# State-space blocks with rows ordered (channel, token) instead of (token, channel), in an encoder trunk on one core

## The chip, the core and the metric

The kernel runs on one core of a Trainium2 chip. The core has a matrix engine (PE), a vector engine (DVE), a scalar engine (ACT), a general engine (POOL) and a sync engine (SP) that issues nearly all DMAs here. The metric is the time of one execution on the device in microseconds (us); lower is better. Every time below is from executions of the kernel before.

## What is computed

Two layers over 512 tokens of width 1024, in float32. Layer 0 is dilated-window attention, layer 1 a bidirectional S5 state-space layer; each is followed by a SwiGLU feed-forward block, and a last norm ends it. The change lies in the state-space layer (64 groups of 16 channels, 64 complex states in each direction):

```python
u = (hn @ w_in).astype(jnp.float32).reshape(b, s, SSM_GROUPS, SSM_GROUP_CH)
y = d_skip.astype(jnp.float32).reshape(SSM_GROUPS, SSM_GROUP_CH) * u
for direction in range(SSM_DIRS):
    y = y + s5_direction(u, a_re[direction], a_im[direction], log_dt[direction], ...,
                         reverse=(direction == 1))
y = jax.nn.gelu(y.reshape(b, s, SSM_WIDTH)).astype(hn.dtype)
ag = y @ w_glu
return ag[..., :D_MODEL] * jax.nn.sigmoid(ag[..., D_MODEL:])
```

`s5_direction` computes `bur, bui = einsum(u, B-bar)`, runs the recurrence `x[t] = lambda x[t-1] + bu[t]` over the tokens and returns `Re(C x)`.

## The kernel before

**Large products.** Every weight matrix is cut into units of 128 output columns. A unit is loaded into `wraw` (SP, L88, L93 or L96) and split into a rounded high part `whi` (ACT, L116) and a remainder `wlo` (L117, on DVE, or on POOL in the state-space stage). A product is then three matmuls per block of 128 x 128 weights: xhi with whi, xlo with whi, xhi with wlo, 24 for a unit of eight blocks. `wraw`, `whi` and `wlo` have three buffers each; loads run three units ahead and splits two. Eight units, those of `w_ssm_in`, are listed in `swap`: they are split with their 128 columns exchanged from (group, channel) to (channel, group), so both instructions (L113, L114) read `wraw` with a step of 16 elements, 64 bytes.

**Tables of the state-space layer.** While PE multiplies the first feed-forward block (FFN0: gps and ups are its gate and up products, fps its output), the class `Tables` builds, for each of the eight tiles T of 128 channels (8 groups), what the state-space stage needs: Ti (input table), ph (phases), Bt (output table) and Mt (the part within a block of 8 tokens). They are cut into pieces; a planner (`Bg`) hands pieces out between the FFN0 matmuls by due time, and all of an engine's work stays in the order in which it was written. `elem_in` (L440 to L442, on DVE) makes `Tn`, the product of powers `pin` (in SBUF, laid out as 8 steps l by 2 by 64 groups) and `bbP` (in PSUM), three instructions of 512 elements for each part: 2 for the halves s of a tile, 2 for real and imaginary part, 8 tiles, 32 sets. Line L440 puts its result in SBUF, L441 in PSUM. `tr_in` (L470) transposes Tn on PE, and the result goes to DRAM (`TinD`, L489). `elem_out` and `elem_ph` run on POOL, `elem_z` on ACT, and `band` (L479 to L484) makes the block for Mt, stored by four DMAs into `MD` (L501). In FFN0, DVE also works for the products themselves: g and u (L1198, L1200, L1202), hl (L1206), wlo; ACT makes g's activation (L1199) and hh (L1205).

**The state-space stage** (about 1030 to 1180 us). A product sps per tile T (24 matmuls), then: `s_u` multiplies sps by the norm factors into `u` (DVE, L1415); `s_move` moves u into the buffer `U` (SP, L1419), which holds 128 rows, one for each token l of a block of 8 and each of 16 channels, by 8 groups by 64 blocks j; `s_v` is 32 small matmuls V, four for each group (L1308); `s_scan` multiplies by ph, scans and multiplies again (DVE L1326 to L1339, POOL L1328 and L1340); ACT copies the state x (L1350, L1352); `s_out` is yps, with Mt on U (L1373) and Bt on x (L1375); then gelu, transposes and the products with w_glu. U has three buffers, u two. SP's queue holds, in one written order, the U transfers, the tables of the coming tiles (`load_tab`, L1251) and the weights. Each DMA of SP takes the next of eight lanes and waits for the one eight before it.

The rows of U are ordered (l, c) with l falling: `s_move` makes one DMA for each l, from all 128 partitions of u (64 elements each) to 16 partitions of U, all groups. With the columns of w_ssm_in exchanged, u's partitions are (c, g).

Of the kernel before, what the change touches and what calls it, by code (L numbers as in the profile page):

```python
# [7 lines left out]
F32 = mybir.dt.float32  # L8
# [62 lines left out]
class WStream:  # L71


    def __init__(self, k, units, swap, pool, la, sa):
        self.k, self.units, self.swap, self.pool, self.la, self.sa = k, units, swap, pool, la, sa
        self.nl = self.ns = self.n = 0
        self.raw, self.hl = {}, {}
        self.lo_engine = k.nc.vector
# [21 lines left out]
    def split_to(self, n):  # L100
        nc = self.k.nc
        while self.ns <= min(n, len(self.units) - 1):
# [6 lines left out]
            if self.ns in self.swap:  # L109

                src = w.rearrange("p a (g c) -> p a c g", c=16)
                h4, l4 = (t.rearrange("p (a c g) -> p a c g", a=a, c=16) for t in (hv, lv))
                nc.scalar.activation(out=h4, in_=src, func=ACTF.Copy)  # L113
                self.lo_engine.tensor_tensor(out=l4, in0=src, in1=fv(h4), op=ALU.subtract)  # L114
            else:
                nc.scalar.activation(out=hv, in_=wv, func=ACTF.Copy)  # L116
                self.lo_engine.tensor_tensor(out=lv, in0=wv, in1=fv(hv), op=ALU.subtract)  # L117
# [63 lines left out]
class Tables:  # L181
# [5 lines left out]
    def __init__(self, k, a, cst, ident, pool, dram, rho):  # L187
# [8 lines left out]
        self.MD = [dram.tile([8, 16, 8, 128], F32, name=f"MD{t}") for t in range(KT)]  # L196
# [236 lines left out]
    def elem_in(self, T, s, i):  # L433
# [3 lines left out]
        if i == 0:  # L437
            self.Tn[T, s] = self.t("Tn", [2, 4, 8, 16], 2)
        t, o = self.ptm.tile([P, 4, 8, 16], F32, tag="tm", name="tm"), self.Tn[T, s][:, i]
        tt(out=o, in0=self.bc(self.pin, 0, g0), in1=self.ch(bb[:, i]), op=ALU.mult)  # L440
        tt(out=t, in0=self.bc(self.pin, 1, g0), in1=self.ch(bb[:, 1 - i]), op=ALU.mult)  # L441
# [21 lines left out]
    def tr_in(self, T, s, q):  # L463
# [4 lines left out]
        for g in range(2):  # L468
            for i in range(2):
                nc.tensor.transpose(ps[:, g, i, :], self.Tn[T, s][:, i, 2 * q + g].rearrange("p l c -> p (l c)"), self.ident)  # L470
# [26 lines left out]
    def store_e(self, T, s):  # L497

        for k_ in range(4):
            e = self.E[32 * k_:32 * k_ + 16, :]  # L500
            self.nc.sync.dma_start(out=self.MD[T][:, :, 4 * s + k_, :].rearrange("l c x -> c l x"),  # L501
# [40 lines left out]
def build(tc, a, out):  # L542
# [45 lines left out]
    swap = range(len(units), len(units) + KT)  # L588
# [31 lines left out]
    with ExitStack() as ctx:  # L620
# [4 lines left out]
        ws = WStream(k, units, swap, wpool, 3, 2)  # L625
# [620 lines left out]
        def load_tab(T, *names):  # L1246
            for n in names:
                shape, src = {"Ti": ([8, 2, 128], tabs.TinD[T]), "ph": ([2, S], tabs.PhD[T]), "Bt": ([2, 8, 128], tabs.BD[T]),
                              "Mt": ([8, 128], tabs.MD[T].rearrange("l c g x -> (l c) g x"))}[n]
# [163 lines left out]
        def s_u(T, ps, rB):  # L1413
            us[T] = sp.tile([P, S], F32, tag="u", name="u", bufs=2)
            nc.vector.tensor_tensor(out=us[T], in0=ps, in1=rB, op=ALU.mult)  # L1415
# [224 lines left out]
```

## Time and profile of the kernel before

| what | us |
|---|---|
| median of 3 runs | 1630.33 |
| range of the runs | 1623.66 to 1632.44 |
| the profiled execution | 1624.28 |
| its span in the trace | 1622.4 |
| PE busy in it | 1527.7 |
| DVE, ACT, POOL busy | 976.6, 660.6, 452.5 |

The profile is of one execution; 1.9 us of its time lie outside the span. The mean granted clock of PE is 0.979 of full speed. Busy time is an average over very different stages, so a change is read from the stretch that it touches: the idle time of PE there, the instruction that ended it, and the instructions that this one waited for in turn. Names such as `wlo<-wraw,whi` give output and inputs; L117 is a line of the kernel before.

### The profile page before, as it was taken

What the parts mean: (1) busy time and instruction counts of PE and PEld (TensorE: products, weight loads), DVE (VectorE), ACT (ScalarE), POOL (GpSimd) and SP (SyncE); (2) the same over time, 40 slices, a digit from 0 to 9 for tenths busy, and PEclk for the clock granted to TensorE, in tenths of its full rate; (3) what the DMA queues carried; (4) which work ended last, traced back from release to release, by engine and by line L of the source; (5) the groups of instructions that cost most, each with busy time, mean ns of one, the idle gap of its engine ahead of it and who ended that gap; (6) DMA issues with size and microseconds to landing.
All of it is one profiled execution on the core that took longest, in us unless ns stands there. A gap on an engine that the chain in (4) does not pass through costs nothing. (4 is left out here: it accounts for less than half of the span.)

```text
span 1622.4 us, 22425 instructions
## 1 busy us (share of the span) xinstructions
PE 1527.7 (94%) x8428; PEld 1261.1 (78%) x8428; DVE 976.6 (60%) x1721; ACT 660.6 (41%) x1172; POOL 452.5 (28%) x535
## 2 busy tenths in 40 slices
PE   8999999999998889799999999887799999999997
PEld 6887888898897668677777777776587888888886
DVE  6366665665666478888578875486547443344234
ACT  5265454454564323244344444442433333233122
POOL 1022001010110250387666754464413101101010
PEclk9999999999999899999999999998999999999999
DMA  6322232231222033355566547467623332333332
GB/s 185 91 78 58 62 92 64 78 87 58 90 68 66 29 86 91 84 143 146 166 194 175 163 145 253 146 223 218 210 70 88 104 103 80 104 98 98 105 102 65
DMA packets 279180, 185.16 MB, mean 114 GB/s; under 512 B 39936, under 2 KB 261280, under 8 KB 277024
## 3 DMA queue, kind: packets, MB, share of 16 engines
q1 hardware_dynamic: 278640, 183.13, 38.3%
q8 instruction: 66, 1.08, 0.3%
q10 hardware_dynamic: 432, 0.60, 0.1%
q14 instruction: 42, 0.34, 0.1%
HBM read 154.34 MB, written 27.26 MB: 112 GB/s over the span
## 5 line engine op out<-in xcount | busy, mean ns | idle before, releaser
L117 DVE TENSOR_TENSOR wlo<-wraw,whi 128x1024 fp32r<-128x1024 f32 (+1 forms) x232 | 312.1, 1349 | 192.7 <-ACT whi L116 191.0
L116 ACT ACTIVATE whi<-wraw 128x1024 fp32r<-128x1024 f32 x238 | 241.1, 1018 | 236.1 <-PE ops L1599 74.3
L789 PE MATMUL gps<-xhi,whi 128*128 128x512 f32 x792 | 320.2, 404 | 9.5 <-DVE hl L1206 6.5
L789 PE MATMUL gps<-xhi,wlo 128*128 128x512 f32 x792 | 311.9, 394 | 7.0 <-DVE wlo L117 7.0
L789 PE MATMUL gps<-xlo,whi 128*128 128x512 f32 x792 | 310.6, 392 | 0.5 <-DVE xlo L649 0.5
L983 POOL COPY st<-st 32x4 f32<-32x4 f32 x256 | 59.7, 233 | 453.9 <-ACT P L971 337.9
L789 PEld LDWEIGHTS gps<-xhi,wlo 128*128 128x128 f32 x792 | 149.3, 189 | 43.7 <-DVE wlo L117 11.2
L789 PEld LDWEIGHTS gps<-xhi,whi 128*128 128x128 f32 x792 | 149.6, 189 | 39.7 <-ACT whi L116 10.0
L789 PEld LDWEIGHTS gps<-xlo,whi 128*128 128x128 f32 x792 | 149.9, 189 | 26.0 <-DVE xlo L649 0.8
L789 PE MATMUL ups<-xhi,wlo 128*128 128x512 f32 x352 | 138.1, 392 | 2.0 <-DVE wlo L117 2.0
L789 PE MATMUL ups<-xhi,whi 128*128 128x512 f32 x352 | 139.6, 397 | 0.0
L789 PE MATMUL ups<-xlo,whi 128*128 128x512 f32 x352 | 137.7, 391 | 0.0
L971 ACT ACTIVATE P<-P,st 128x256 f32<-128x256 f32 x128 | 63.8, 499 | 68.7 <-DVE st L968 68.6
L1202 POOL TENSOR_TENSOR u<-u,g 128x512 f32<-128x512 f32 x22 | 28.4, 1291 | 209.7 <-DVE u L1200 202.2
L789 PEld LDWEIGHTS ups<-xhi,wlo 128*128 128x128 f32 x352 | 66.4, 189 | 17.0 <-DVE wlo L117 2.8
L452 POOL TENSOR_TENSOR B<-pout,C 128x512 f32<-128x512 f32 x32 | 45.3, 1415 | 122.4 <-DVE pout L178 64.3
L789 PEld LDWEIGHTS ups<-xhi,whi 128*128 128x128 f32 x352 | 66.5, 189 | 14.5 <-issue 1.2
L789 PEld LDWEIGHTS ups<-xlo,whi 128*128 128x128 f32 x352 | 66.6, 189 | 13.4
L1199 ACT ACTIVATE g<-g 128x512 f32<-128x512 f32 x44 | 27.7, 630 | 115.2 <-DVE g L1198 115.2
L789 PE MATMUL fps<-hh,whi 128*128 128x512 f32 x176 | 71.4, 406 | 3.4 <-ACT hh L1205 2.7
L891 PE MATMUL vps<-whi,xhi 128*128 128x256 f32 x256 | 73.3, 286 | 0.0
L1205 ACT ACTIVATE hh<-u 128x512 fp32r<-128x512 f32 x44 | 27.8, 633 | 109.9 <-POOL u L1202 87.7
(303 smaller groups left out, 3163.1 us busy)
## 6 DMA issues: line engine op xcount, KB each, us to landing
wraw<-in_w_ffn_in SPq DMA_DIRECT2D x88, 512.0 KB, 3.8
wraw<-in_w_qkv SPq DMA_DIRECT2D x72, 512.0 KB, 3.6
wraw<-in_w_ffn_out SPq DMA_DIRECT2D x38, 512.0 KB, 4.0
BD<-B SPq DMA_DIRECT2D x16, 512.0 KB, 5.3
TinD<-Tt SPq DMA_DIRECT2D x16, 512.0 KB, 3.5
Ti<-TinD SPq DMA_DIRECT2D x8, 1024.0 KB, 6.0
Bt<-BD SPq DMA_DIRECT2D x8, 1024.0 KB, 7.3
wraw<-in_w_attn_out SPq DMA_DIRECT2D x8, 512.0 KB, 3.8
```

Source lines behind the costliest of these rows:

```text
L116: nc.scalar.activation(out=hv, in_=wv, func=ACTF.Copy)
L117: self.lo_engine.tensor_tensor(out=lv, in0=wv, in1=fv(hv), op=ALU.subtract)
L452: tt(out=B[:, i], in0=self.bc(self.pout, i, g0), in1=self.ch(C[:, 0]), op=ALU.mult)
L789: nc.tensor.matmul(dst, w[:, kt, :], x, start=(start and kt == ks[0] and j == 0), stop=(stop and kt == ks[-1] and j == 2))
L891: nc.tensor.matmul(ps[rp][:, r % 2, :], x, w[:, kk, :], start=(kt == 0 and j == 0 and r % 2 == 0), stop=(kt == 7 and j == 2 and r % 2 == 1))
L971: nc.scalar.activation(out=Pt[:, j, :], in_=Pt[:, j, :], func=ACTF.Exp, bias=st[:, 32 + off + j:33 + off + j], accum_out=st[:, 8 + off + j ...
L983: nc.gpsimd.tensor_copy(par[32 * z:32 * z + 32, y, :, :], own[32 * y:32 * y + 32, z, :, :])
L1199: nc.scalar.activation(out=g, in_=g, func=ACTF.Silu)
L1202: eng.tensor_tensor(out=u, in0=u, in1=g, op=ALU.mult)
L1205: nc.scalar.activation(out=hi, in_=u, func=ACTF.Copy)
```

## The change

The rows of U, of Ti and of Mt go from (l, c) to (c, l).

- The columns of w_ssm_in keep their order: `swap` is gone, and all units are split by the contiguous instructions. The partitions of u are then (g, c).
- `s_u` writes u with the eight blocks of 64 tokens in reverse, by a negative step between blocks; still one instruction.
- `s_move` makes one DMA for each group g: from 16 partitions of u (8 blocks of 64 elements each) to all 128 partitions of U at that group. Again eight DMAs of 32 KB in pieces of 256 bytes for a tile.
- `elem_in` makes Tn as (group, c, l). pin is read with l as the inner index, 128 elements (512 bytes) apart, and each set is repeated for the 16 c; bbP is repeated for the 8 l. Before, pin was repeated for c (inner) and bbP read along c.
- `MD` is laid out (c, l), so `store_e` writes 128 rows of 512 bytes in order; `load_tab` reads Mt accordingly.

The diff, without the places where the parameter `swap` is passed on:

```diff
@@ -106,15 +106,8 @@
             lo = self.pool.tile([P, 1024], F32R, tag="wlo", name="wlo")
             hv, lv = (t[:, 0:a * b] for t in (hi, lo))
             wv = w.rearrange("p a b -> p (a b)")
-            if self.ns in self.swap:
-
-                src = w.rearrange("p a (g c) -> p a c g", c=16)
-                h4, l4 = (t.rearrange("p (a c g) -> p a c g", a=a, c=16) for t in (hv, lv))
-                nc.scalar.activation(out=h4, in_=src, func=ACTF.Copy)
-                self.lo_engine.tensor_tensor(out=l4, in0=src, in1=fv(h4), op=ALU.subtract)
-            else:
-                nc.scalar.activation(out=hv, in_=wv, func=ACTF.Copy)
-                self.lo_engine.tensor_tensor(out=lv, in0=wv, in1=fv(hv), op=ALU.subtract)
+            nc.scalar.activation(out=hv, in_=wv, func=ACTF.Copy)
+            self.lo_engine.tensor_tensor(out=lv, in0=wv, in1=fv(hv), op=ALU.subtract)
             self.hl[self.ns] = tuple(t.rearrange("p (a b) -> p a b", a=a) for t in (hv, lv))
             self.ns += 1
 
@@ -193,7 +186,7 @@
         self.TinD = [dram.tile([P, 8, 2, 128], F32, name=f"TinD{t}") for t in range(KT)]
         self.BD = [dram.tile([P, 2, 8, 128], F32, name=f"BD{t}") for t in range(KT)]
         self.PhD = [dram.tile([P, 2, S], F32, name=f"PhD{t}") for t in range(KT)]
-        self.MD = [dram.tile([8, 16, 8, 128], F32, name=f"MD{t}") for t in range(KT)]
+        self.MD = [dram.tile([16, 8, 8, 128], F32, name=f"MD{t}") for t in range(KT)]
         self.z, self.C = {}, {}
 
     def scratch(self, n, cols):
@@ -435,10 +428,13 @@
         g0 = 8 * T + 4 * s
         bb = self.bbP[:, :, 4 * s:4 * s + 4]
         if i == 0:
-            self.Tn[T, s] = self.t("Tn", [2, 4, 8, 16], 2)
-        t, o = self.ptm.tile([P, 4, 8, 16], F32, tag="tm", name="tm"), self.Tn[T, s][:, i]
-        tt(out=o, in0=self.bc(self.pin, 0, g0), in1=self.ch(bb[:, i]), op=ALU.mult)
-        tt(out=t, in0=self.bc(self.pin, 1, g0), in1=self.ch(bb[:, 1 - i]), op=ALU.mult)
+            self.Tn[T, s] = self.t("Tn", [2, 4, 16, 8], 2)
+        t, o = self.ptm.tile([P, 4, 16, 8], F32, tag="tm", name="tm"), self.Tn[T, s][:, i]
+
+        pw = [self.pin[:, :, j, g0:g0 + 4].rearrange("p l (g o) -> p g o l", o=1).to_broadcast([P, 4, 16, 8]) for j in range(2)]
+        b = [bb[:, j].rearrange("p g (c o) -> p g c o", o=1).to_broadcast([P, 4, 16, 8]) for j in range(2)]
+        tt(out=o, in0=pw[0], in1=b[i], op=ALU.mult)
+        tt(out=t, in0=pw[1], in1=b[1 - i], op=ALU.mult)
         tt(out=o, in0=o, in1=t, op=(ALU.subtract, ALU.add)[i])
 
     def elem_out(self, T, s):
@@ -467,7 +463,7 @@
         ps = self.psb.tile([P, 2, 2, 128], F32, tag="b", name="tps")
         for g in range(2):
             for i in range(2):
-                nc.tensor.transpose(ps[:, g, i, :], self.Tn[T, s][:, i, 2 * q + g].rearrange("p l c -> p (l c)"), self.ident)
+                nc.tensor.transpose(ps[:, g, i, :], self.Tn[T, s][:, i, 2 * q + g].rearrange("p c l -> p (c l)"), self.ident)
         nc.scalar.activation(out=self.Tt[:, 2 * q:2 * q + 2], in_=ps, func=ACTF.Copy)
 
     def band(self, T, s):
@@ -498,7 +494,7 @@
 
         for k_ in range(4):
             e = self.E[32 * k_:32 * k_ + 16, :]
-            self.nc.sync.dma_start(out=self.MD[T][:, :, 4 * s + k_, :].rearrange("l c x -> c l x"),
+            self.nc.sync.dma_start(out=self.MD[T][:, :, 4 * s + k_, :],
                                    in_=bass.AP(tensor=e.tensor, offset=e.offset, ap=[list(e.ap[0]), [16, 8], [1, 128]]))
 
     def pieces(self):
@@ -1246,7 +1241,7 @@
         def load_tab(T, *names):
             for n in names:
                 shape, src = {"Ti": ([8, 2, 128], tabs.TinD[T]), "ph": ([2, S], tabs.PhD[T]), "Bt": ([2, 8, 128], tabs.BD[T]),
-                              "Mt": ([8, 128], tabs.MD[T].rearrange("l c g x -> (l c) g x"))}[n]
+                              "Mt": ([8, 128], tabs.MD[T].rearrange("c l g x -> (c l) g x"))}[n]
                 t = tbx2[0].tile([P] + shape, F32, tag=n, name=n, bufs=2)
                 nc.sync.dma_start(out=t, in_=src)
                 ld.setdefault(T, {})[n] = t
@@ -1412,11 +1407,16 @@
 
         def s_u(T, ps, rB):
             us[T] = sp.tile([P, S], F32, tag="u", name="u", bufs=2)
-            nc.vector.tensor_tensor(out=us[T], in0=ps, in1=rB, op=ALU.mult)
-
-        def s_move(T, lo_=0, hi_=8):
-            for l in range(lo_, hi_):
-                nc.sync.dma_start(out=Us[T % 3][112 - 16 * l:128 - 16 * l, :, 1:65], in_=us[T][:, 64 * l:64 * l + 64])
+            u = us[T]
+            v = lambda x: x.rearrange("p (l j) -> p l j", l=8)
+
+            nc.vector.tensor_tensor(out=bass.AP(tensor=u.tensor, offset=u.offset + 448, ap=[list(u.ap[0]), [-64, 8], [1, 64]]),
+                                    in0=v(ps), in1=v(rB), op=ALU.mult)
+
+        def s_move(T):
+
+            for g in range(8):
+                nc.sync.dma_start(out=Us[T % 3][:, g, 1:65], in_=us[T][16 * g:16 * g + 16].rearrange("c (l j) -> c l j", l=8))
 
         ws.lo_engine = nc.gpsimd
         late = []
```

What this does to the order of work. On PE, at the V matmuls of tile T = 1 (they read U and Ti), the kernel before has this; DMAHW0 to 7 are SP's eight lanes:

```order
L789 MATMUL sps_9704<-xlo_9456,whi 128x512
L789 MATMUL sps_9704<-xhi_9455,wlo 128x512
L1308 MATMUL V<-U_9485,Ti 64x64 [waits DMAHW3_49,DMAHW4_49,DMAHW2_49,DMAHW5_49,DMAHW1_49,DMAHW6_49,DMAHW0_49,DMAHW7_49,DVE_49,PE_49]
L1308 MATMUL V<-U_9485,Ti 64x64 x31
L1373 MATMUL yps<-Mt,U_9484 64x128 x2
```

and the changed kernel this:

```order
L784 MATMUL sps_9704<-xlo_9456,whi 128x512
L784 MATMUL sps_9704<-xhi_9455,wlo 128x512
L1303 MATMUL V<-U_9485,Ti 64x64 [waits DMAHW3_49,DVE_49,PE_49]
L1303 MATMUL V<-U_9485,Ti 64x64 x3
L1303 MATMUL V<-U_9485,Ti 64x64 [waits DMAHW4_49]
L1303 MATMUL V<-U_9485,Ti 64x64 x3
```

One wait for eight transfers at the first matmul has become a wait for one transfer ahead of each group's four matmuls; 28 of the tile's 32 matmuls can run before its last transfer has landed.

On SP, at the transfers of u into U for tile T = 3, the first that use a U buffer again (yps of T = 0, on PE, has to have read it), the kernel before has:

```order
L1251 DMA ph<-PhD_5475 128x1024 [waits DMAHW6_49,DVE_49]
L1419 DMA U_9484<-u 16x8x64 [waits DMAHW7_49,DVE_49,PE_49]
L1419 DMA U_9484<-u 16x8x64 [waits DMAHW0_49]
L1419 DMA U_9484<-u 16x8x64 [waits DMAHW1_49]
L1419 DMA U_9484<-u 16x8x64 [waits DMAHW2_49]
```

and the changed kernel:

```order
L1246 DMA ph<-PhD_5475 128x1024 [waits DMAHW6_49,DVE_49]
L1419 DMA U_9484<-u 128x1x64 [waits DMAHW7_49,DVE_49,PE_49]
L1419 DMA U_9484<-u 128x1x64 [waits DMAHW0_49,PE_49]
L1419 DMA U_9484<-u 128x1x64 [waits DMAHW1_49,PE_49]
L1419 DMA U_9484<-u 128x1x64 [waits DMAHW2_49,PE_49]
L1419 DMA U_9484<-u 128x1x64 [waits DMAHW3_49]
L1419 DMA U_9484<-u 128x1x64 [waits DMAHW4_49]
L1419 DMA U_9484<-u 128x1x64 [waits DMAHW5_49]
L1419 DMA U_9484<-u 128x1x64 [waits DMAHW6_49,PE_49]
L1246 DMA Mt<-MD_5483 128x1024 [waits DMAHW7_49]
```

Before, the first transfer waits for PE and the others for their lanes alone; after, transfers 0 to 3 and 7 each wait for PE's reads of their own group. The loads of Mt and of what follows stand in the same place behind them.

## Rows read from the trace of the kernel before

**Rows 1.** The page, part 1: busy us (share of the span) and instructions, by engine.

```profile
PE 1527.7 (94%) x8428; PEld 1261.1 (78%) x8428; DVE 976.6 (60%) x1721; ACT 660.6 (41%) x1172; POOL 452.5 (28%) x535
```

**Rows 2.** Table by stretches: start:end, length, busy us by engine, clock, DMA share, GB/s.

```profile
690.00:1000.00 310.00, 299.69 (x1529) 233.13 (x1529) 237.26 (x284) 136.28 (x248) 207.67 (x140) 0.99 0.58 164
853.00:966.00 113.00, 107.26 (x554) 83.44 (x554) 93.39 (x113) 49.75 (x92) 77.98 (x52) 1.00 0.57 159
1150.00:1180.00 30.00, 22.45 (x156) 18.43 (x157) 12.53 (x14) 14.06 (x22) 13.61 (x8) 0.83 0.53 144
```

**Rows 3.** Waits of PE, 680 to 1000 us: total us, times, longest us.

```profile
PE gps L789 <- DVE hl L1206: 6.5, 1, 6.5
PE gps L789 <- DVE wlo L117: 4.6, 5, 1.7
```

**Rows 4.** Timeline of PE: start, length, instruction, idle time before it and its releaser.

```profile
853.34 0.50 PE L789 MATMUL gps<-xhi,wlo 128*128 128x512 f32 x1 [0.40 <-DVE wlo L117]
...
966.12 0.50 PE L789 MATMUL fps<-hh,whi 128*128 128x512 f32 x1 [2.75 <-ACT hh L1205]
```

**Rows 5.** Waits of DVE, 819 to 967 us, and below from 689 to 819 us.

```profile
DVE u L1202 <- ACT g L1199: 9.9, 4, 2.5
DVE hl L1206 <- ACT hh L1205: 7.7, 11, 0.7
DVE wlo L117 <- ACT whi L116: 5.2, 9, 1.2
...
DVE wlo L117 <- ACT whi L116: 29.8, 12, 6.4
```

**Rows 6.** Groups of DVE by line, 819 to 966.1 us: busy us, mean ns, idle before.

```profile
L440 DVE TENSOR_TENSOR Tn<-pin,bbP 128x512 f32<-128x512 f32 x16 | 10.8, 678 | 0.0
L441 DVE TENSOR_TENSOR tm<-pin,bbP 128x512 f32<-128x512 f32 x16 | 11.0, 687 | 0.0
```

**Rows 7.** Single lines: count, then nanoseconds min/median/max, first and last start, forms.

```profile
L113 ACT ACTIVATE whi<-wraw x8: 1916/2008/2032, 1021.9 to 1083.3; 128x1024 fp32r<-128x1024 f32 x8
...
L114 POOL TENSOR_TENSOR wlo<-wraw,whi x6: 2860/2900/2921, 1033.2 to 1089.3; 128x1024 fp32r<-128x1024 f32 x6
L114 DVE TENSOR_TENSOR wlo<-wraw,whi x2: 1960/1968/1977, 1023.9 to 1027.1; 128x1024 fp32r<-128x1024 f32 x2
...
L117 DVE TENSOR_TENSOR wlo<-wraw,whi x232: 548/1225/2486, 16.9 to 1598.2; 128x1024 fp32r<-128x1024 f32 x100, 128x384 fp32r<-128x384 f32 x16
...
L412 POOL TENSOR_TENSOR ph<-AB x16: 1459/1582/2452, 681.5 to 983.5; 128x512 f32<-128x512 f32 x16
...
L452 POOL TENSOR_TENSOR B<-pout,C x32: 1102/1159/2176, 672.0 to 961.3; 128x512 f32<-128x512 f32 x32
```

**Rows 8.** Waits of PE from 1000 to 1180 us.

```profile
PE yps L1375 <- ACT x L1352: 17.8, 12, 5.3
PE pe L789 <- ACT gpart L1479: 7.6, 1, 7.6
PE rsps L672 <- DVE rcol L667: 0.7, 1, 0.7
```

**Rows 9.** Timelines of PE and DVE around the first V.

```profile
1050.08 3.49 PE L1308 MATMUL V<-U,Ti 128*64 128x64 f32 x64 [3.46 <-DMA U<-u]
...
1050.25 0.69 DVE L1415 TENSOR_TENSOR u<-sps,rsB 128x512 f32<-128x512 f32 x1 [6.49 <-DMA U<-u]
1053.60 0.69 DVE L1326 TENSOR_TENSOR t<-V,ph 128x512 f32<-128x512 f32 x1 [2.66 <-PE V L1308]
```

**Rows 10.** Waits of SP, DVE and ACT, 1000 to 1180 us, and the U transfers' line.

```profile
SPq L1419 <- PE yps L1373: 4.9, 1, 4.9
...
DVE t L1326 <- DMA ph<-PhD: 16.6, 4, 7.5
...
ACT whi L116 <- DMA wraw<-in_w_glu: 31.1, 4, 13.1
...
L1419 SPq DMA_DIRECT2D U<-u x64: 547/597/1647, 1043.2 to 1140.5; - x64
```

More of the change, by code (lines that the diff above doesn't have):

```diff
@@ L71, with __init__ @@
 class WStream:
-    def __init__(self, k, units, swap, pool, la, sa):
-        self.k, self.units, self.swap, self.pool, self.la, self.sa = k, units, swap, pool, la, sa
+    def __init__(self, k, units, pool, la, sa):
+        self.k, self.units, self.pool, self.la, self.sa = k, units, pool, la, sa
         self.nl = self.ns = self.n = 0
@@ L587, in build @@
             units.append(col(a["w_ffn_out"][0], m * 128, 128, half * HALF + 8, HALF - 8))
-    swap = range(len(units), len(units) + KT)
     for m in range(KT):
@@ L624, in build @@
         ctx.enter_context(tc.manual_schedule())
-        ws = WStream(k, units, swap, wpool, 3, 2)
+        ws = WStream(k, units, wpool, 3, 2)
         cst = left.tile([P, NCONST], F32, name="cst")
```

## Prediction

> **What bounds the kernel now.** The page comes first: TensorE (PE) is busy 94% of the span and DVE, the next, 60% [rows 1]. So a change gains where PE stands idle and loses where it makes PE idle. The table by stretches says where that is [rows 2]. The change touches two places: FFN0 up to 1000 us, beside which the state-space tables are built, and the state-space stage, about 1030 to 1180 us. From 690 to 1000 us PE is busy 299.69 of 310 us. In the second stage it is busy 22.45 of the 30 us from 1150 on, at a granted clock of 0.83.
>
> The sums of waits then name what PE lacks. Around FFN0 it is one wait of 6.5 us for DVE's hl and five for DVE's wlo, 4.6 us [rows 3], and smaller ones; two of the stalls are shown where they stand [rows 4]. In the state-space stage PE waits 17.8 us for the state x from ACT, 7.6 us for gpart, 0.7 us before rsps [rows 8], and 3.46 us before the first V for U's transfers [rows 9]: 29.6 us in all. Behind x and gpart stands a chain over other engines: DVE waits 16.6 us for the table ph and ACT 31.1 us for w_glu, whose loads both stand in SP's queue, and SP itself waits 4.9 us for yps to release a U buffer [rows 10]. So that stage is paced by SP's queue about as much as by DVE.
>
> **Part 1, the exchange of columns goes.** The eight units of w_ssm_in are split by contiguous instructions. A swapped unit took 1.968 us on DVE against 1.225 for a plain one, 0.74 us less for each of two units; POOL's six took 2.900 and ACT's eight 2.008 us [rows 7], and I take about the same saving for these. No unit of them is waited for by PE from 1000 us on [rows 8], so nearly all of it lies beside PE's work. What it can give directly is the 0.7 us before rsps, since DVE's rcol chain stands behind two of these subtractions. I count 0.7 us, and ends of 0 and 0.7.
>
> **Part 2, U by groups.** Before, the first V matmul of each T waits for all eight U transfers; after, the four matmuls of each group wait for that group's transfer. A batch is eight transfers of 32 KB in 256-byte pieces either way, and one issue takes 0.6 us on SP [rows 10]. At T = 0 the V matmuls start at 1050.08 and run 3.49 us [rows 9]. After, seven eighths of them, 3.49 x 7/8 = 3.05 us, run while later transfers land. DVE's t follows V [rows 9], but u(2) of 0.69 us now meets it and takes 0.4 us back. With the 0.7 of part 1 that is 3.05 + 0.7 - 0.4 = **3.4 us**, the lower end of what this stage gains if the transfers cost the same.
>
> The upper end is SP's. Before, the first transfer of U(3) waits until yps(0) has read the whole buffer (4.9 us [rows 10]); after, transfers 0 to 3 and 7 wait for their own group, as the order shows. U(3) then goes out while yps(0) runs, and the loads of Mt, Bt, w_ssm_in, Ti, ph and w_glu queued behind it go out up to 4.9 + 3.4 = 8.3 us earlier. Who waits for these is DVE (ph, 16.6 us) and ACT (w_glu, 31.1 us). What is late next: DVE's own work, and the load lanes, in which each transfer waits for the one eight before it. I put the upper end at 10 us, a third of PE's 29.6 us of waiting, and take **6.5 us**, about the middle, since two of the four waits (V and x) are moved directly. No row of before shows a transfer from 16 partitions to 128; the nearest, the present one, issues in 0.547 to 1.647 us, median 0.597 [rows 10]. I take no extra cost because count and size of the pieces stay; at +0.2 us an issue, SP would carry 64 x 0.2 = 12.8 us more in this stage, at -0.2 as much less.
>
> **Part 3, Tin's rows in the order (c, l).** The first two instructions of every set in elem_in, L440 and L441, now read pin with an inner step of 128 elements (512 bytes), where the same element was repeated over c. There are 64 of them (8 T, 2 halves, 2 parts, 2 each), at 0.678 and 0.687 us [rows 6]. No row shows this read on DVE. The nearest is DVE's subtraction with an input at a 64-byte step: 1.968 against 1.225 us for 1024 elements [rows 7], 0.726 ns per element, 0.37 us for 512. On POOL, elem_ph has the same 512-byte inner step and a median of 1.582 us against 1.159 for elem_out with the repeated element [rows 7], both beside DVE's traffic: a factor 1.36, or 0.25 us on 0.68. Bounds: 0 (the operand in PSUM may set the pace already) and 0.6 us (the step is eight times that of the DVE row). I take 0.37 us, the same engine and the nearest kind of read, so 64 x 0.37 = 24 us of DVE work.
>
> A rule speaks against this edit. The Trainium skill, page "SBUF — State Buffer", section "Door 1: The DMA port swizzle (why `[64,N]` ≈ `[32,N]`)", says that SBUF has lines of 16 bytes and that an access which moves on to a new line pays a penalty; it gives no size. By it the new read of pin pays on each element, and the DVE pair above (1.968 against 1.225 us) agrees; if it held for no operand beside PSUM, the sum would be that of rival (a).
>
> How much of the 24 us reaches PE? From 819 to 967 us DVE never waits for PE or a transfer: all its idle time is behind ACT's g, hh and whi [rows 5], and g and hh in turn follow DVE's own results. PE is stalled by DVE's wlo at 853.34 and, through hh, at 966.12 [rows 4], so lateness of DVE is handed to PE one to one. In that stretch there are 16 + 16 such instructions [rows 6]: 32 x 0.37 = 11.8 us. DVE's 5.2 us behind whi [rows 5] could absorb a little, where whi's own cause is a load; I take off a tenth, 0.5 us. Two more instructions stand ahead of the hl for which PE waits 6.5 us [rows 3]: 0.7 us. Sum 11.8 - 0.5 + 0.7 = **+12.0 us**. The other 30 instructions (from 688 to 812 us and behind 974) lie where DVE stands idle anyway (29.8 us behind whi from 689 to 819 us [rows 5], some 1.1 us for each of the 26 instructions there, since ACT's split waits for buffers that PE frees), and cost nothing; without that cover they are 30 x 0.37 = 11 us more. The ends for 0 and 0.6 us an instruction are 0 and 32 x 0.6 - 0.5 + 1.2 = 19.9 us. The clock there reads 1.00 with PE idle 5.7 of 113 us [rows 2], so I add nothing for it.
>
> **Part 4, at nothing.** Tn's transposes stay contiguous; the 64 stores of MD still move 128 pieces of 512 bytes each and stand in SP's queue behind a wait for DVE; u is still one instruction of 512 elements in runs of 64. No engine's order changes. If the reversed blocks of u cost 0.37 us like a strided read, eight of them are 3 us of DVE beside V.
>
> **Sum.** +12.0 - 6.5 = +5.5 us on the profiled execution of 1624.28 us. That one lies 6 us below the median of 1630.33 (runs from 1623.66 to 1632.44), so the difference is put on the median: **1635.8 us**.
>
> **Rivals.**
> (a) The new read is free beside an operand in PSUM. For: L440, with one operand in PSUM, and L441, with two, take nearly the same time [rows 6], so something else than the operands' layout may set it. Against: DVE's and POOL's pairs [rows 7]. Then only the gain counts, -3.4 to -10: 1620.3 to 1626.9 us, and with the 6.5 taken above **1623.8 us**.
> (b) Slower, by DVE's pace from 819 to 966 us: 0.6 us an instruction and only 3.4 us of gain, 19.9 - 3.4 = +16.5, **1646.8 us**. It decides from 0.45 us on: 32 x 0.45 - 0.5 + 0.9 - 6.5 = +8.3. For: DVE is busy 93.39 of 113 us there and the rest is spent behind ACT [rows 2, 5]. Against: POOL's pair gives less.
> (c) The order of U by groups does not do what it says beyond T = 0, because DVE or the lanes hold the rest: 12.0 - 3.4 = +8.6, **1638.9 us**. For: DVE waits for ph four times only [rows 10].
> (d) The U transfers issue 0.2 us slower and half of the 12.8 us reaches PE: +5.5 + 6.4 = +11.9, **1642.2 us**.
>
> **Chances.** A measurement of this kernel can tell about 0.5%, 8.1 us, from no change. The forecast has 0.37: 0.29 of it within that bound, 0.04 faster (the full gain of 10 and lateness that other idle time takes up) and 0.04 slower. (a) has 0.36, since no row shows the new read itself; half of that is beyond -8.1. (b) has 0.11, all slower; (c) 0.11, of which 0.06 slower; (d) 0.05, slower. Faster by over 0.5%: 0.04 + 0.18 = 0.22; slower: 0.04 + 0.11 + 0.06 + 0.05 = 0.26; within: the other 0.52. For eight in ten the range reaches from the better end of (a) to nearly the price of (b): 1619 to 1646 us; the forecast's own runs from 1629 to 1639.
>
> **What would show it.** L440 and L441 at about 1.05 us: at 0.68 it is (a), above 1.13 (b). PE's waits for wlo and hh between 819 and 966 us about 11 us longer, and the stall of 966.12 near 978. In the state-space stage the matmuls of V(0) spread over the landings with no single wait of 3.5 us; SP's wait for yps before U(3) gone or split; DVE's wait for ph below 16.6 and ACT's for w_glu below 31.1 us; the stretch from the first sps to the last x shorter by 3.4 to 10 us. I am wrong if FFN0's end does not move, if the U transfers issue or land slower, or if PE's waits for x do not shrink.

## The result: slower by 0.85%, with nearly twice the forecast loss and a gain about as forecast

| kernel | median us | lowest to highest | n |
|---|---|---|---|
| before | 1629.44 | 1623.66 to 1632.44 | 5 |
| changed | 1640.86 | 1637.46 to 1645.82 | 5 |

The ratio is 1.0085 with an interval of 1.0064 to 1.0107: 11.4 us slower, where 5.5 were forecast. The profiled execution of the changed kernel has a span of 1635.6 us, 13.2 more than that of before. In later sets before had medians of 1623.97 to 1627.32 and the changed kernel, measured again, 1643.02 (ratio 1.0122, 1.0105 to 1.0139), so its loss is 11 to 19 us.

To compare executions, each trace is cut at three instructions that every kernel has: the stall of PE for wlo near 688 to 694 us (A), its first sps matmul (S), and the start of the last group of eight yps matmuls of the state-space stage (G). A to S is called FFN0, S to G the stage.

| execution | A | S | G | FFN0 | stage | S to the end of the first V | G to the end |
|---|---|---|---|---|---|---|---|
| before | 688.68 | 1027.15 | 1177.75 | 338.5 | 150.6 | 26.4 | 444.7 |
| changed | 688.50 | 1048.59 | 1190.09 | 360.1 | 141.5 | 22.0 | 445.5 |

So FFN0 lost 21.6 us, the stage gained 9.1, and 0.8 were lost behind it.

**The rows of FFN0.** The table by stretches, A to S, before and then after (columns as in [rows 2]):

```profile
688.68:1027.15 338.47, 327.01 (x1645) 255.41 (x1646) 252.52 (x300) 149.51 (x264) 217.10 (x147) 0.99 0.61 178
```

```profile
688.50:1048.59 360.09, 337.43 (x1644) 260.63 (x1645) 273.80 (x300) 147.89 (x264) 215.91 (x147) 0.96 0.58 167
```

DVE has the same 300 instructions and is busy 273.80 instead of 252.52 us: 21.3 us more, and the stretch is 21.6 us longer. The added time is in the two edited lines, now L436 and L437 (count, then nanoseconds min/median/max):

```profile
L436 DVE TENSOR_TENSOR Tn<-pin,bbP x32: 1017/1072/1237, 679.8 to 997.6; 128x512 f32<-128x512 f32 x32
...
L437 DVE TENSOR_TENSOR tm<-pin,bbP x32: 1014/1073/1117, 680.7 to 998.6; 128x512 f32<-128x512 f32 x32
```

They answer to [rows 6]: 1.072 and 1.073 us against 0.678 and 0.687. What PE waits for, summed from A to S of the changed kernel (total us, times, longest), answers to [rows 3, 4]:

```profile
PE fps L784 <- ACT hh L1200: 4.5, 1, 4.5
PE gps L784 <- DVE wlo L110: 4.2, 4, 1.8
PE fps L784 <- DVE wlo L110: 4.1, 5, 1.5
PE gps L784 <- ACT whi L109: 4.0, 2, 3.3
PE fps L784 <- ACT whi L109: 3.0, 5, 1.4
PE tps L466 <- DVE Tn L438: 2.4, 2, 2.2
```

New among them is the wait for Tn. The others stood there before, 4.6 us for wlo at gps and the rest shorter:

```profile
PE fps L789 <- DVE wlo L117: 2.9, 3, 1.1
PE fps L789 <- ACT hh L1205: 2.7, 1, 2.7
PE gps L789 <- ACT whi L116: 1.2, 1, 1.2
```

Of the 21.6 us, 11.2 are more idle time of PE (338.47 - 327.01 = 11.46 before, 360.09 - 337.43 = 22.66 after) and 10.4 are longer busy time, at a lower clock; more on the clock below. The stall for hh, at 966.12 us before [rows 4], is here:

```profile
985.65 0.79 PE L784 MATMUL fps<-hh,whi 128*128 128x512 f32 x1 [4.46 <-ACT hh L1200]
```

**The rows of the stage.** The first V no longer waits 3.46 us in one piece [rows 9]. It waits four times for single transfers, the first of them being

```profile
1068.20 0.45 PE L1303 MATMUL V<-U,Ti 128*64 128x64 f32 x8 [0.17 <-DMA U<-u]
```

and the sums that answer to [rows 8, 10] are, of PE, DVE, ACT and SP from 1030 us on:

```profile
PE yps L1370 <- ACT x L1347: 14.0, 10, 3.8
PE pe L784 <- ACT gpart L1479: 8.1, 1, 8.1
...
DVE t L1321 <- DMA ph<-PhD: 9.4, 3, 5.9
...
ACT whi L109 <- DMA wraw<-in_w_glu: 28.5, 4, 13.5
...
SPq L1419 <- PE yps L1368: 3.9, 6, 0.9
```

PE's waits for x fell from 17.8 to 14.0 us and DVE's for ph from 16.6 to 9.4; those for w_glu (31.1 to 28.5) and gpart (7.6 to 8.1) hardly moved.

### The profile page after: what moved, and what is told of

It reads as the page before. It is cut to its first block, busy times and chain, and to the rows that moved or that the text cites. A ratio compares the mean times of both kernels' runs of the same rounds, so it can differ in the third digit from the quotient of the medians.

```text
span 1635.6 us, 22423 instructions
## 1 busy us (share of the span) xinstructions
PE 1536.5 (94%) x8428; PEld 1264.8 (77%) x8428; DVE 993.7 (61%) x1721; ACT 653.6 (40%) x1172; POOL 448.3 (27%) x535
## 5 line engine op out<-in xcount | busy, mean ns | idle before, releaser
L109 ACT ACTIVATE whi<-wraw 128x1024 fp32r<-128x1024 f32 x246 | 249.6, 1019 | 254.4 <-PE ops L1599 74.3
L784 PE MATMUL gps<-xhi,whi 128*128 128x512 f32 x792 | 323.4, 408 | 12.3 <-ACT whi L109 11.3
L784 PE MATMUL gps<-xhi,wlo 128*128 128x512 f32 x792 | 315.2, 398 | 6.7 <-DVE wlo L110 6.6
L784 PEld LDWEIGHTS gps<-xhi,whi 128*128 128x128 f32 x792 | 151.6, 191 | 43.4 <-ACT whi L109 13.3
L448 POOL TENSOR_TENSOR B<-pout,C 128x512 f32<-128x512 f32 x32 | 42.0, 1311 | 135.7 <-ACT C L394 71.4
L784 PE MATMUL fps<-hh,wlo 128*128 128x512 f32 x176 | 70.2, 399 | 4.1 <-DVE wlo L110 4.1
```

Source lines behind the costliest of these rows:

```text
L448: tt(out=B[:, i], in0=self.bc(self.pout, i, g0), in1=self.ch(C[:, 0]), op=ALU.mult)
L784: nc.tensor.matmul(dst, w[:, kt, :], x, start=(start and kt == ks[0] and j == 0), stop=(stop and kt == ks[-1] and j == 2))
```

## The experiments

### Is it the strided read alone, or the store of MD?

SP's issues of the MD store became dearer, which had been costed at nothing: 0.592 instead of 0.424 us. They stand ahead of the loads of w_ffn_out, and ACT's whi waits longer for these (below). So there were two suspects for FFN0.

```profile
L501 SPq DMA_DIRECT2D MD<-E x64: 313/424/439, 705.2 to 994.1; - x64
```

```profile
L497 SPq DMA_DIRECT2D MD<-E x64: 565/592/1417, 707.9 to 1016.6; - x64
```

**pin with l inner** (`e1_pin_l_inner`): the read is contiguous again, the order of Tn's rows stays changed.

```diff
-        self.pin, self.pout = self.t("pin", [8, 2, 64]), self.t("pout", [8, 2, 64])
+        self.pin, self.pout = self.t("pin", [2, 64, 8]), self.t("pout", [8, 2, 64])
+        pv = self.pin.rearrange("p j g l -> p l j g")
...
-        pw = [self.pin[:, :, j, g0:g0 + 4].rearrange("p l (g o) -> p g o l", o=1)...
+        pw = [self.pin[:, j, g0:g0 + 4].rearrange("p (g o) l -> p g o l", o=1)...
```

> The changed kernel with the powers pin stored with l as the inner index (written with a step of 8 elements by eight short instructions of the parameters), so that elem_in reads them in a row; all else as in the changed kernel. Theory 1, the strided read alone makes FFN0 late (64 x 0.39 = 25 us of DVE, handed to PE in part directly, in part through SP's queue): the two instructions fall from 1.07 to about 0.68 us, the stall of PE that is at 966 us before and at 985.7 after is back within 2 us of 966, and the time is the one of before less the gain of the state-space stage, about 1629.4 - 8 = 1621 us. Rival 2, the stores of MD in their new form (0.592 against 0.424 us an issue, 64 x 0.168 = 10.8 us of SP) make the loads of w_ffn_out late: that stall stays at about 976 and the time is about 1631 us.

Measured: 1624.43 us, ratio to before 0.9987 (0.9972 to 1.0002). The two lines are back at 0.680 and 0.689 us, and FFN0 is 344.8 us: 15.3 of the 21.6 us are gone. The single line, the stretch, and the stall for hh:

```profile
L437 DVE TENSOR_TENSOR Tn<-pin,bbP x32: 674/680/687, 684.2 to 987.4; 128x512 f32<-128x512 f32 x32
...
692.92:1037.67 344.75, 329.55 (x1644) 257.08 (x1645) 254.23 (x300) 147.72 (x264) 217.03 (x147) 0.98 0.60 175
...
976.24 0.50 PE L785 MATMUL fps<-hh,whi 128*128 128x512 f32 x1 [3.00 <-ACT hh L1201]
```

Two marks of the expectation were missed. The stall stands at 976.24 us, which is the rival's mark and not 966; but A is 4.2 us later in this execution, and measured from A the stall is at 283.3 us, against 277.4 before and 297.1 in the changed kernel. And the time is 3 us below before, within the noise, where 8 were expected.

**MD in its old order** (`e2_md_old`), with the read still strided:

```diff
-        self.MD = [dram.tile([16, 8, 8, 128], ...
+        self.MD = [dram.tile([8, 16, 8, 128], ...
...
-            self.nc.sync.dma_start(out=self.MD[T][:, :, 4 * s + k_, :],
+            self.nc.sync.dma_start(out=self.MD[T][:, :, 4 * s + k_, :].rearrange("l c x -> c l x"),
...
-                              "Mt": ([8, 128], tabs.MD[T].rearrange("c l g x -> (c l) g x"))}[n]
+                              "Mt": ([8, 128], tabs.MD[T].rearrange("l c g x -> c l g x"))}[n]
```

> The changed kernel with MD kept in DRAM in the order (l, c) as before, stored by the DMA of before (16 x 8 x 128) and put into the order (c, l) by the load of Mt. Theory 1: issue falls to 0.42 us, and the time stays at about 1641 us (within 3). Rival 2: about 10 us faster, 1631 us, and ACT's waits for w_ffn_out between 690 and 820 us fall from 26 to below 20 us.

Measured: 1644.35 us, ratio 1.0106 (1.0089 to 1.0124); FFN0 is 360.0 us, as with the dear store, though the issue is back at 0.423; ACT's waits for w_ffn_out from 690 to 825 us are 23.2 us, not below 20:

```profile
L497 SPq DMA_DIRECT2D MD<-E x64: 312/423/1456, 710.9 to 1019.0; - x64
```

**Both edits** (`e3_pin_md`):

> Both edits together: pin with l inner and MD in its old order. Theory 1: as with pin alone, about 1621 us. Rival 2: 1621 us too, but faster than pin alone by about 10 us. If the two only add up, this is the faster of all.

Measured: 1626.88 us, ratio 1.0001 (0.9987 to 1.0016), FFN0 341.3 us. The 1621 us were not reached, and the two edits don't add up.

**The strided read alone, in the kernel before** (`e4_before_strided`):

```diff
-        tt(out=o, in0=self.bc(self.pin, 0, g0), in1=self.ch(bb[:, i]), op=ALU.mult)
-        tt(out=t, in0=self.bc(self.pin, 1, g0), in1=self.ch(bb[:, 1 - i]), op=ALU.mult)
+        cl = lambda x: x.rearrange("p g l c -> p g (l c)").rearrange("p g (c l) -> p g c l", l=8)
+        tt(out=cl(o), in0=pw[0], in1=b[i], op=ALU.mult)
+        tt(out=cl(t), in0=pw[1], in1=b[1 - i], op=ALU.mult)
```

(pw and b as in the change.)

> The kernel before with one part of the change: the two first instructions of elem_in read pin with l inner (512-byte step) and make the rows of Tn in the order (c, l); the rest of the kernel keeps the order (l, c), so what the state-space layer computes is not the layer. Theory 1: all of FFN0's loss appears, the stall of 966 moves to about 985, and the time is 1629.4 + 20 = about 1649 us, as none of the state-space stage's gain is there. Rival 2: half of it, 1639 us.

Measured: 1647.98 us against 1627.32 of before in that set, ratio 1.0121 (1.0103 to 1.0140), +20.7 us; FFN0 359.3 us, 20.8 more than before, with the old store.

```profile
692.29:1051.59 359.30, 334.08 (x1645) 257.55 (x1645) 274.43 (x300) 149.46 (x264) 216.10 (x147) 0.97 0.57 167
```

The four runs settle it: the strided read by itself makes the loss of FFN0, and of the 10 us that the rival gave to the store's dearer issue nothing is seen. A few us of it can't be excluded, since FFN0 varies: in `e5_group0_last` (below), whose edit doesn't touch FFN0, it is 363.7 us, 3.6 more than in the changed kernel.

```profile
692.54:1056.27 363.73, 336.55 (x1644) 259.24 (x1645) 279.55 (x300) 147.80 (x264) 212.95 (x147) 0.96 0.57 166
```

DVE's busy time and the length of the stretch go up together (252.52, 273.80, 274.43 and here 279.55 us; 338.5, 360.1, 359.3 and 363.7).

### Why DVE's idle time was no cover

64 x 0.39 = 25 us were added and 21.6 arrived. What is missing was not covered by idle time. From A to S, DVE is idle for 86.0 us before (338.47 - 252.52) and 86.3 after (360.09 - 273.80). Of the 64 instructions 62 lie there and take 24.7 us more; DVE's other instructions take 3.4 us less in sum, and 21.3 are left. Why those are shorter is not shown.

The forecast had counted 30 of the 64 instructions as covered, since DVE waits 29.8 us for whi from 689 to 819 us [rows 5]. The same instructions set side by side in both traces show the lateness in that stretch: 0.9 us at 692, 2.7 at 705, 5.65 at 744, then steady to 760, 8.3 at 775, 10.3 at 792 and 11.2 at 813 us. What ACT, the maker of whi, waits for there tells why; from 690 to 820 us, first before, then after:

```profile
ACT bb L431 <- DVE bbP L218: 17.9, 3, 6.1
ACT whi L116 <- DMA wraw<-in_w_ffn_out: 17.4, 4, 6.5
ACT g L1199 <- DVE g L1198: 13.1, 5, 4.9
ACT whi L116 <- PE fps L789: 8.7, 2, 8.1
```

```profile
ACT whi L109 <- DMA wraw<-in_w_ffn_out: 26.3, 6, 8.4
ACT g L1194 <- DVE g L1193: 18.8, 5, 5.8
ACT bb L424 <- DVE bbP L211: 18.5, 3, 6.4
```

ACT does its work in the order in which it was written. A whi that DVE waits for stands behind ACT's copy bb, which waits 17.9 us in sum for DVE's bbP. So before, DVE's bbP begins at 752.73 us, ACT's bb at 753.07, whi behind it at 756.05, and DVE's wlo at 756.59 after 3.55 us of idle time. Up to about 760 us DVE's idle time is therefore mostly a wait for DVE's own work, one engine removed, and a later DVE makes no use of it. From 763 us on whi waits for w_ffn_out's loads, 17.4 us before and 26.3 after. These loads stand in SP's queue behind the MD and Tin stores, which wait for DVE's E and ACT's Tt. SP's wait for E, from 740 to 820 us before, and then one set of stores with the whi that waits for the load behind it, before and after:

```profile
SPq L501 <- DVE E L484: 25.1, 4, 8.3
```

```profile
768.56 1.76 SPq L501 DMA_DIRECT2D MD<-E  x4
...
774.51 1.06 ACT L116 ACTIVATE whi<-wraw 128x1024 fp32r<-128x1024 f32 x1 [5.80 <-DMA wraw<-in_w_ffn_out]
```

```profile
775.89 2.53 SPq L497 DMA_DIRECT2D MD<-E  x4
...
782.80 1.06 ACT L109 ACTIVATE whi<-wraw 128x1024 fp32r<-128x1024 f32 x1 [8.44 <-DMA wraw<-in_w_ffn_out]
```

The stores begin 7.3 us later, and whi 8.3. That way DVE's lateness comes back through SP. The runs bear it out: from 690 to 825 us, ACT waits for these loads 24.2 us with the strided read and the cheap store (`e4_before_strided`), and 8.8 with the contiguous read and the dear store (`e1_pin_l_inner`). So the wait follows the read. No run changed this route alone.

The clock has no visible part in it. The changed kernel was profiled once more, unchanged (`e12_after_again`):

> The changed kernel, unchanged, profiled once more. Two executions of the kernel before agree in FFN0 (338.5 and 338.0 us from PE's wlo stall near 690 us to the first sps) and differ by 4.5 us in the state-space stage (150.6 and 146.1 us from there to the last yps), since DVE's wait for ph differs by 3.9 us. If the stage's gain is one of the change, it is again 141 to 144 us here; if the 9 us between the two first executions are mostly chance, 145 us or more. FFN0 within 1 us of 360.1.

Its FFN0 is 360.1 us again, with a higher clock and less busy time on PE:

```profile
692.04:1052.11 360.07, 332.84 (x1644) 256.50 (x1645) 272.75 (x300) 147.68 (x264) 214.79 (x147) 0.98 0.58 167
```

PE is busy 332.84 here and 337.43 us in the first execution, at clocks of 0.98 and 0.96, and the stretches agree to 0.02 us. In both, PE ran at half clock right behind its stall for hh; the first has five places with a lowered clock, the second three. The one behind the stall of 985.65 in the first:

```profile
986.00:990.00 4.00, 4.00 (x12) 2.94 (x12) 1.86 (x3) 3.90 (x9) 0.00 (x0) 0.50 0.90 285
```

PE's idle time is 22.7 us in the first and 27.2 in the second: where DVE sets the pace, a slower PE only waits less.

### What the stage's gain is made of

First, how far the stage can be read at all. The kernel before, profiled once more (`e11_before_again`):

> The kernel before, unchanged, profiled once more, to see by how much the two stretches differ between two executions of one kernel: under 1 us each if a difference of 2 us between the kernels is one of the kernels; FFN0 340 us or more if the 2.8 us by which the run with pin and MD old is longer than before are chance.

FFN0 is 338.0 us, within half a microsecond; the stage is 146.1 instead of 150.6 us. Instruction by instruction the two executions keep within half a microsecond of each other on DVE as far as about 1100 us; the difference appears at DVE's t of 1108 us, which waits 7.47 us for the load of ph in one and 3.54 in the other. The sums for the second execution of before (its first has 16.6 us [rows 10]) and for the second of the changed kernel (its first has 9.4):

```profile
DVE t L1326 <- DMA ph<-PhD: 11.6, 4, 6.7
```

```profile
DVE t L1321 <- DMA ph<-PhD: 8.9, 3, 5.6
```

The stage of before is 150.6, 146.1 and, with the strided read added, 148.2 us; that of the changed kernel 141.5 and 140.9. The gain is about 7 us (148.3 - 141.2), with 4 to 5 us of play in any single pair. Up to the end of the first V there is hardly any: 26.4, 26.5 and 26.6 us from S with the old order, 22.0 twice with the new. So 4.4 us of gain are firm at that mark; the rest, behind the first V, is 119.6 to 124.2 us against 119.5 and 118.9 and can't be told from play.

**V by groups** (`e5_group0_last`): group 0's transfer is sent last, so V's first matmul waits for all.

```diff
-            for g in range(8):
+            for g in (1, 2, 3, 4, 5, 6, 7, 0):
                 nc.sync.dma_start(out=Us[T % 3][:, g, 1:65], ...
```

> The changed kernel with the eight U transfers of a tile sent in the order of groups 1 to 7 and then 0, while V still begins with group 0: the first V matmul waits for the last transfer, so V by groups is gone; U's buffer is still released by groups. Stage length = from PE's wait for wlo in the last fps product to its last wait for x in yps: 162.7 us before, 154.3 after. Theory: V by groups is worth 3 of these 8.4 us, V(0) waits some 3.4 us again and the stage is 157 to 158 us. Rival, it is worth nothing beyond T = 0 and the rest of the stage takes it up: 154 to 155 us.

Measured: 1644.04 us; by the mark of the expectation 156.9 us, from S on a stage of 144.0, and 25.1 us from S to the end of the first V instead of 22.0. The wait is back:

```profile
1077.98 2.29 PE L1303 MATMUL V<-U,Ti 128*64 128x64 f32 x38 [3.35 <-DMA U<-u]
```

That is 3.1 us at the first V, as the forecast had it: for the first V the theory holds. At the end of the stage 2.5 are left (144.0 against 141.5; 156.9 against 154.3 by the other mark), which is less than the play there.

**Release by groups** (`e6_group7_first`): the same line with `(7, 0, 1, 2, 3, 4, 5, 6)`.

> The changed kernel with the U transfers in the order of group 7 and then 0 to 6: group 7 is read last by yps, so the first transfer again waits until yps has read the whole buffer and U's release by groups is gone; V still waits by groups (its first matmul for the second transfer). Theory: the early release is worth about 5 of the 8.4 us, stage 158 to 160 us, and SP's wait for yps before U(3) is near 5 us in one piece. Rival, SP's early release is used up in its other waits: 154 to 156 us.

Measured: 1642.66 us; 154.2 us by the mark of the expectation, from S on 142.3, so 0 to 0.8 us more than the changed kernel, though SP waits again in one piece:

```profile
SPq L1419 <- PE yps L1370: 5.9, 2, 5.0
```

The theory's 4 to 6 us more are not there, as the rival had it; a gain of a microsecond or two from the early release can't be excluded, given the play. SP's timeline of U(3), before and after (start, length of the group of issues), says why:

```profile
1068.68 5.71 SPq L1419 DMA_DIRECT2D U<-u  x8
```

```profile
1082.49 10.53 SPq L1419 DMA_DIRECT2D U<-u  x8
```

It starts 11.9 us behind the end of the first V instead of 15.1, but takes 10.5 us instead of 5.7, and ends 22.4 behind it instead of 20.8. yps reads groups q and q + 4 together in its quarter q, so group 3 is read in the last quarter, and the fourth transfer waits for that with four more behind it. But it issues at 1086.71 us, and the last two only at 1090.81 and 1092.48. What SP waits for at these, from 1082 to 1094 us of the changed kernel:

```profile
SPq L1419 <- PE yps L1368: 2.1, 3, 0.7
SPq L1419 <- DMA Ti<-TinD: 1.9, 1, 1.9
SPq L1419 <- DMA ph<-PhD: 1.1, 1, 1.1
```

The seventh and eighth transfer take the lanes of the loads of Ti and ph, issued at 1081.16 and 1081.81 and landed at 1090.80 and 1092.42, and can't go out before. Even the first transfer, issued at 1082.49, lands at 1092.70, right behind ph; before, it was issued 5.5 us behind ph and landed 0.2 us behind it. So what was issued earlier didn't land earlier.

**The order of release** (`e10_group_order`) takes the wait for group 3 out: groups go 0 4 1 5 2 6 3 7 in the transfers and in V, on top of pin with l inner and the store of e9.

> The kernel of the run above with the groups of a tile taken in the order in which yps frees them, 0 4 1 5 2 6 3 7, in the U transfers and in V. In the changed kernel U(3)'s eight transfers take 10.5 us on SP, since the fourth waits for group 3, which yps reads in its last quarter, and four more stand behind it. Theory: two transfers instead of five remain after yps' last quarter, SP is 2 us earlier for each tile and the stage is 142 us. Rival, SP's time there is not on the path any more: 144 us.

Measured: 1624.96 us, ratio 0.9998 (0.9985 to 1.0010), stage 142.3 against 142.0 us of e9: no gain, although the 142 us of the theory were met. The sixth of U(3)'s transfers goes out 15.8 us behind the end of the first V instead of 17.8, as meant, but all eight still take 10.65 us, since the seventh waits for its lane. From 1071 to 1083 us:

```profile
SPq L1424 <- DMA Ti<-TinD: 3.6, 1, 3.6
```

SP was not 2 us earlier, so the run doesn't say what that would be worth.

**The splits of w_ssm_in** (`e7_swap_back`): the removed branch of `split_to` is put back into the changed kernel.

> The changed kernel with the eight units of w_ssm_in split by the reads at a 64-byte step again (the columns of u are then exchanged, so what the state-space layer computes is not the layer). Theory: these splits lie beside other work and cost 0.7 to 1.5 us: stage 155 to 156 us. Rival, POOL's longer subtractions delay its t and with it the whole chain: stage 158 us or more, and DVE waits over 3 us more for POOL's t.

Measured: 1640.38 us; 154.8 us by the mark of the expectation, from S on 142.9, so 0.5 to 1.4 us more than the changed kernel; at the end of the first V it is 1.2 us (23.2). DVE's wait for POOL's t is 3.7 us in sum instead of 3.2, not the rival's 3 us more. The wait of [rows 8] before rsps is back:

```profile
1064.19 1.16 PE L675 MATMUL rsps<-cst,rcol 128*128 128x128 f32 x8 [0.67 <-DVE rcol L670]
```

At the end of the first V, V by groups (3.1) and the splits (1.2) make 4.3 of the 4.4 us gained there. By the stage's end the single runs give 2.5, 0.5 to 1.4 and, for the release, 0 to 0.8 us, each within the play of the stage; the rest of the 7 us is play or was not found.

### What makes the store dear, and is there a better version?

**An empty row in MD** (`e8_pin_l_pad`), so that the rows of a store can't be merged:

```diff
+        self.MD = [dram.tile([16, 9, 8, 128], ...
+            self.nc.sync.dma_start(out=self.MD[T][:, 0:8, 4 * s + k_, :],
+                              "Mt": ([8, 128], tabs.MD[T][:, 0:8].rearrange("c l g x -> c l g x"))}[n]
```

> pin with l inner as before, and MD in the order (c, l) with one empty row behind each 8 (16 x 9 x 8 x 128), so that the rows of a store can't be merged into one dimension of 128 and both sides of the DMA have the form 16 x 8 x 128; the load of Mt then has the form 16 x 8 on its DRAM side. Theory: it is the differing form of the two sides that costs SP 0.592 instead of 0.424 us an issue: 0.42 here, FFN0 as in the run with pin and MD in its old order (PE's stall for hh some 280 us behind its stall for wlo at 688.7), time about 1625. Rival, it is the DRAM order (c, l): 0.59 us an issue and FFN0 3 us longer, about 1627 us.

Measured: 1627.16 us, ratio 1.0022 (1.0010 to 1.0033), FFN0 341.1 us, stage 145.8.

```profile
L498 SPq DMA_DIRECT2D MD<-E x64: 312/423/1369, 709.4 to 999.5; - x64
```

The issue is 0.423 us in the order (c, l), so it isn't the order in DRAM. **The store with l falling on both sides** (`e9_pin_l_rev`) was to have that without the empty row:

```diff
+            self.nc.sync.dma_start(out=bass.AP(tensor=d.tensor, offset=d.offset + 7 * 1024 + 128 * (4 * s + k_),
+                                               ap=[[8192, 16], [-1024, 8], [1, 128]]),
+                                   in_=bass.AP(tensor=e.tensor, offset=e.offset + 112, ap=[list(e.ap[0]), [-16, 8], [1, 128]]))
```

> pin with l inner, and MD in the order (c, l) stored with l falling on both sides, so that DRAM rows can't be merged and the store has the form 16 x 8 x 128 on both sides, while the load of Mt stays one of 128 whole rows. Stretches: FFN0 = from PE's stall for wlo near 688 to 694 us to its first sps matmul (338.5 us before, 360.1 after, 344.8 with pin alone, 341.3 with pin and MD old); state-space stage = from that matmul to the last yps matmul (150.6, 141.5, 143.9, 145.9). Theory, the store's form costs FFN0 3.5 us and the load's form costs the stage 2 us, and neither is paid here: 0.42 us an issue, 341 and 144 us, time about 1622 us, some 0.3% faster than before. Rival, the 2 us of the stage are chance: 341 and 146 us, 1624 us.

Measured: 1626.76 us, ratio 1.0009 (0.9993 to 1.0025), FFN0 341.9 us, stage 142.0. Half of the theory failed: the issue is dear although the program has the form 16 x 8 x 128 on both sides,

```profile
L499 SPq DMA_DIRECT2D MD<-E x64: 575/593/1405, 708.9 to 1000.4; - x64
```

so what costs 0.17 us is either rows that follow each other in DRAM or, here, the negative step. And FFN0 is short with the dear issue (341.9), while it is 344.8 and 344.5 us in e1 and e10 with the same one: the store is not the cause of these 3 us either. e9 and e10 have the same instructions up to the stage, and their FFN0 differs by 2.7 us all the same, so 3 us are within what FFN0 varies between executions. The three kernels whose Mt load is in two dimensions (e2, e3, e8) have stages of 144.8 to 145.9 us, the others with the change 140.9 to 144.0, which fits a dearer load of Mt but is within the play of the stage.

With the stride gone, the five versions lie between 0.9987 and 1.0022 of before. The lowest, pin with l inner, is some 16 to 22 us faster than the changed kernel by their ratios to before and can't be told from before (0.9972 to 1.0002). Its stage (143.9 us) is 4.4 us shorter than before's mean. FFN0 is 341.1 to 344.8 us in these five against 338.0 and 338.5 before, 3 to 7 us longer, for a reason that stays open.

## Why the prediction came out as it did

- **The read's price was right.** 0.37 us an instruction were taken from DVE's pair at a 64-byte step [rows 7]; measured are 1.072 - 0.678 = 0.39 and 1.073 - 0.687 = 0.39 us, at a step of 512 bytes and with an operand in PSUM. Rival (a), that it is free, fell, and so did the price of rival (b). The rule of the Trainium skill (page "SBUF — State Buffer", section "Door 1: The DMA port swizzle (why `[64,N]` ≈ `[32,N]`)") gave the right sign. The size, which it doesn't give, is nearly the same per element at both steps here: 0.73 and 0.76 ns.
- **The step that failed is "cost nothing" for the 30 instructions from 688 to 812 us and behind 974.** The lateness at 813 us is 11.2 us where 0.7 were summed, and 1.9 us more arise between the hh stall and S where nothing was. (The 0.7 themselves, ahead of the 6.5 us stall, don't show: that stall is 6.47 us before and 6.48 after.) DVE's idle time behind whi was read as cover because "ACT's split waits for buffers that PE frees". That is 8.7 us of ACT's waits from 690 to 820 us; 17.9 are the copy bb waiting for DVE's own bbP, and 17.4 are loads that stand behind stores of DVE's E. The prediction had priced this failure (30 x 0.37 = 11 us more), and its sum with it, 12 + 11 = 23 us, is what FFN0 lost within 2 us; it gave the case no chance of its own.
- **From 819 to 966 us the one-to-one passage was nearly right:** 11.3 us were summed, and the lateness went from 11.4 us behind A at the stall of 814 to 19.7 at the stall for hh: 8.3. The 32 instructions took 12.5 us more and DVE's others there 5.8 less, for a reason that no run shows; the sum had no term for that. The sign of 11 us more in PE's waits for wlo and hh did not come: from A to S they are 12.8 us against 10.2, and the rest of PE's loss is waits for whi and Tn and a lower clock.
- **The clock was rightly left out of the sum,** as the second execution shows.
- **The stage: right size, half of the reasons.** 6.5 us were taken; 9.1 in the first pair of traces and about 7 over all. V by groups at T = 0 was 3.05, measured 3.1; part 1 was 0.7, measured 1.2 at the first V. These are firm; that the total came near 6.5 is in part play of the stage. The upper end, SP's early release, did not show: 0 to 0.8 us. The prediction had named "the load lanes" as late next, and it is they that hold U(3), with the time that Ti and ph take to land; which group yps reads when was not looked up.
- **"At nothing" for the stores of MD was wrong as a row** (0.424 to 0.592 us, 64 x 0.17 = 10.8 us of SP) and right as a result, as far as FFN0 can be read: with the old store it is 360.0 us.
- **The U transfers** issue as before (0.589 against 0.597 us), as taken. They land later, 3.4 against 2.6 us from issue in the median, which the prediction had named as a sign of being wrong. It isn't their form: at T = 0 both kinds land in 2.0 to 2.1 us, and it is T = 3, issued earlier behind Ti and ph, that takes 2 to 10 us instead of 2 to 3. Rival (d) did not come about, though its 1642.2 us are nearest to the 1640.86 measured. Rival (c), that the lanes hold what lies beyond T = 0, is close to what the runs show of U, with 4.4 us in place of its 3.4.

The sum was +12.0 - 6.5 = +5.5. With the traces' values it is +21.6 - 9.1 + 0.8 = +13.3 us, the difference of the spans but for rounding; the medians differ by 11.4. 1640.86 us lies inside the stated range of 1619 to 1646 but outside the forecast's own 1629 to 1639: the range holds because it was drawn wide for the rivals' sake.

## What to carry to other kernels

Idle time of an engine is cover only if the wait behind it ends on something that does not depend on that engine. Follow the wait one engine further: if the instruction waited for stands in a queue behind one that waits for the first engine, its idle time is its own work come back, and added work goes to the end, as here. A layout that spares an exchange in one place moves the stride to another; count the elements that are read with a step at both places, and what paces each place, before choosing where it stands.

## What the runs showed of the hardware that was not expected

- DVE's price for a stepped read in float32 is nearly the same at 64 and at 512 bytes: 0.73 ns per element (1.968 against 1.225 us for 1024) and 0.76 (1.073 against 0.68 to 0.69 us for 512), the second with the other operand in PSUM.
- A half clock of PE behind a stall cost nothing where DVE set the pace: FFN0 took 360.09 us with PE busy 337.43 us and 360.07 us with 332.84.
- The issue of a DMA on SP depends on its form: 0.42 us for 16 x 8 rows of 512 bytes with a gap in DRAM or in the order (l, c), 0.59 us where the 128 rows follow each other at one distance and also where 16 x 8 rows are taken backwards on both sides. What the form changes is open.
- A small transfer issued earlier behind large loads didn't land earlier: the first of U(3), 32 KB, landed 0.2 to 0.3 us behind ph's load both when it was issued 0.7 us behind that load (1081.81 to 1082.49) and when it was issued 5.5 us behind it (1063.19 to 1068.68).
